# Second MLP products of a fp32 encoder: one of four weight sums and part of the common additions moved from VectorE to accumulating DMAs, and the third sum's split placed a pass earlier

## The chip, the cores and the metric

The kernel runs on one core of a Trainium2 chip. The metric is the device time of one execution in microseconds. Engines are named as in the profile: PE (TensorE matmul), PEld (its weight loads), DVE (VectorE), ACT (ScalarE), POOL (GpSimd) and SP (SyncE, which here only issues DMAs). DMAs are also issued from POOL's queue; those that accumulate into their destination are all issued there.

## The reference, cut to what matters

```python
D_MODEL = 1024; SEQ = 512; DEPTH = 2; D_FF = 4 * D_MODEL     # two sequences of 512 tokens

def sq_relu_mlp(h, w_up, w_down):
    a = jnp.maximum(h @ w_up, 0)
    return (a * a) @ w_down

def trunk(x, ...):
    for i in range(DEPTH):
        j = i // N_MIXERS
        if i % N_MIXERS == 0:
            x = x + fourier_mix(rms_norm(x, fourier_norm[j]), fourier_w_out[j])
        else:
            x = x + gqa_attention(rms_norm(x, attn_norm[j]), attn_w_qkv[j], attn_q_norm[j],
                                  attn_k_norm[j], attn_w_o[j])
        x = x + sq_relu_mlp(rms_norm(x, mlp_norm[i]), mlp_w_up[i], mlp_w_down[i])
    return rms_norm(x, final_norm)
```

All is float32. The change touches `(a * a) @ w_down`, the second product of the MLP, in both layers.

## The kernel before

**How a product is made.** A float32 matmul is done as three matmuls of float32r operands: each operand is split into an upper part (a cast, on ACT, line L82) and a lower part (value minus upper part, on DVE, line L83). `split`, `halves`, `load_w` and `load_raw` (whose DMA is issued on SP, line L91) do this for weights. `product` (matmuls at line L812) multiplies a 128x512 weight tile, as four k-blocks, with four 128x512 blocks of activations: 4 k-blocks times 3 matmuls, 12 matmuls of 512 columns.

**Seven products for eight.** The two sequences and the two halves of the 1024 outputs make a 2x2 block product, which is computed with seven block multiplications in the manner of Winograd. In `second_product(l, blocks, rows, late, ready)` two of the seven belong to class `Row` (first: weights a11, second: a12) and five to class `Sums`. The five `Sums` products of an output tile m (0 to 3) and a group g of k-blocks are s1·t1, s3·t3, s2·t2, s4·b22 and a22·t4, with weight sums s1 = a21 + a22, s2 = s1 - a11, s3 = a11 - a21, s4 = a12 - s2. The t and b are activation sums that the first product left in DRAM. `Sums.load` loads four weight blocks as two 512 KB transfers (x = a12, a21 and y = a11, a22, each block 128x512). `sum_123` makes s1, s2 and s3 by three DVE operations, L1126 to L1128, s1 and s2 in a buffer s of its own; `split_12`, `sum_4` (L1134), `split_4` and `split_3` follow (`split_3` splits s3 and a22, which stand side by side in y).

**The loop.** Each layer has 16 `items`: a `Sums` and the `Row`s due before it. One turn of the loop, a pass, runs the row's first product if there is one, then s1·t1, s3·t3, the row's second product, s2·t2, s4·b22 and a22·t4. A pass with a row has 84 matmuls, a pass without has 60; in layer 0 the last two passes have no row. After each product DVE adds the PSUM bank to an accumulator (L1059), which frees the bank. Meanwhile the next item is loaded (after s1·t1) and its sums and splits are made (after s2·t2 and s4·b22); only the third sum's split, `split_3`, stands at the start of the item's own pass. In layer 1 the sums of the first group are half as wide.

**What sets the order.** Within the loop only PE's order is the order of the code (`tc.manual_schedule(engines={PE})`); DVE, ACT, POOL and SP are ordered by a scheduler from the order of emission and readiness, and each then runs its own instructions strictly in that order. Raw weights live in 5 buffers of 128x1024 (`rawp`), taken round-robin: a load waits until the buffer's former content has been split or summed. Split weights have 4 buffers (`wp`), activations 38, short-lived tiles 8, PSUM 8 banks.

**The end of an output tile.** `e[m]` is a common part that goes to three of the four output blocks. When the last `Row` or `Sums` of m is through, `finish(m)` adds it: L1223 into the upper half of `xs[0, m]`, L1224 into both halves of `xs[1, m]`. Then `ready(m)` is called. In layer 0 it prepares the attention layer for the two sequences and two halves: `make_h` multiplies by a gain and splits (ACT L86, DVE L87), `square` squares (ACT L157) and adds (POOL L159), `put_away` stores `xs` to DRAM on SP (L186). `late()`, called in each of the last two passes of layer 0, loads and splits pieces of the attention's `w_qkv`. In layer 1 `ready` does nothing. In layer 0 the attention's projections (matmul lines L77 to L79) come after the last pass.

Of the kernel before, what the change touches and what calls it, by code (L numbers as in the profile page):

```python
# [11 lines left out]
F32 = mybir.dt.float32  # L12
# [3 lines left out]
ALU = mybir.AluOpType  # L16
AX = mybir.AxisListType

P = 128
# [21 lines left out]
def trunk_kernel(ctx, tc, x_in, xt_in, y_out, dcos, dsin, feat, rope, gfour, gcol, grow, gfin,  # L41
                 w_four, w_nyq, w_qkv, w_o, w_up, w_row2, w_row4, w_sum2, w_sum4, w_down):
    nc = tc.nc
# [3 lines left out]
    rawp = ctx.enter_context(tc.tile_pool(name="rawp", bufs=5))  # L47
# [9 lines left out]
    def nm(s):  # L57
        n_[0] += 1
        return f"{s}_{n_[0]}"

    def slot(shape, dt):
        return act.tile(shape, dt, tag="u4", name=nm("u"))

    def tm(shape=(P, 512), dt=F32):
        return tmp.tile(list(shape), dt, tag="t2", name=nm("t"))

    def small(n=4):
        return sm.tile([P, n], F32, tag="s", name=nm("s"), padded_shape=[P, 8])
# [20 lines left out]
    def load_raw(src, shape=(P, 1024)):  # L89
        raw = rawp.tile(list(shape), F32, tag="raw", name=nm("raw"))  # L90
        nc.sync.dma_start(raw, src)  # L91
        return raw
# [49 lines left out]
    xs, acc = {}, {}  # L142
# [9 lines left out]
    def square(q, fo, n=512):  # L152

        if fo == 0:
            acc[q] = tm()
        s = tm() if fo else acc[q]
        nc.scalar.activation(s[:, :n], xt(q, fo)[:, :n], AF.Square)  # L157
        if fo:
            nc.gpsimd.tensor_add(acc[q][:, :n], acc[q][:, :n], s[:, :n])  # L159
# [17 lines left out]
    def make_h(q, fo, g0):  # L177

        h = slot([P, 2, 512], F32R)
        split_scaled(h[:, 0], h[:, 1], xt(q, fo), gc[:, g0 + fo : g0 + fo + 1])  # L180
        return h
# [3 lines left out]
    def put_away(q, i):  # L185
        nc.sync.dma_start(park[q, i], xs[q, i])  # L186
# [390 lines left out]
    def even_outs(q, fos):  # L577
        return outs(q, fos, we, 0, 258, (wn.w, un[q]))
# [31 lines left out]
    with tc.manual_schedule(engines={ET.PE, ET.Activation, ET.DVE, ET.Pool, ET.SP}):  # L610
# [138 lines left out]
        for fo in range(KC):  # L749
            e, = even_outs(1, [fo])  # L750
# [289 lines left out]
    def second_product(l, blocks, rows, late=lambda: None, ready=lambda m: None):  # L1040
        e, new = [], [True] * 4
# [11 lines left out]
        def put(op, h):  # L1053
            for hi, lo in h:
                split(hi, lo, f32(lo))
            b[op] = b.get(op, []) + [(hi[:, i], lo[:, i]) for hi, lo in h for i in range(2)]
# [11 lines left out]
        def residual(q, m):  # L1068
            if (q, m) not in there:
                xs[q, m] = slot([P, 2, 512], F32)  # L1070
                nc.sync.dma_start(xs[q, m], park[q, m])
                there.add((q, m))
            return xs[q, m]
# [8 lines left out]
        def sums_raw(m, g, n):  # L1082
            if (1, m, g) in early:
                return early[1, m, g]
            w = w_sum4[3 * l + g, m] if n == 4 else w_sum2[m]
            return [load_raw(w[:, i : i + 2], (P, 2, n * P)) for i in (0, 2)]

        class Row:


            def __init__(self, m, g, n):
                self.m, self.g, self.n = m, g, n

            def load(self):
                residual(0, self.m)
                self.raw = None if self.m in rows_early else row_raw(self.m, self.g, self.n)
# [15 lines left out]
        class Sums:  # L1112


            def __init__(self, m, g, n):
                self.m, self.g, self.n, self.o = m, g, n, {}

            def load(self):
                for q in range(NSEQ):
                    residual(q, self.m)  # L1120
                self.x, self.y = sums_raw(self.m, self.g, self.n)

            def sum_123(self):
                a21, a11, a22 = self.x[:, 1], self.y[:, 0], self.y[:, 1]
                s = self.s = rawp.tile([P, 2, self.n * P], F32, tag="raw", name=nm("raw"))
                nc.vector.tensor_add(s[:, 1], a21, a22)  # L1126
                nc.vector.tensor_sub(s[:, 0], s[:, 1], a11)
                nc.vector.tensor_sub(a11, a11, a21)  # L1128

            def split_12(self):  # L1130
                self.s2, self.s1 = halves(self.s, self.n * P, (own, narrow)[self.n == 2])
# [31 lines left out]
        b, left = {}, [len(steps) // 4] * 4  # L1163
# [55 lines left out]

        def finish(m):  # L1220
            left[m] -= 1
            if left[m] == 0:
                nc.vector.tensor_add(xs[0, m][:, 1], xs[0, m][:, 1], e[m])  # L1223
                nc.vector.tensor_add(xs[1, m], xs[1, m], e[m].unsqueeze(1).broadcast_to([P, 2, 512]))  # L1224
                ready(m)

        first_product(l, blocks, rows, ahead)
        e += [tm() for _ in range(4)]
        items, waiting = [], []
        for _, i, m, g, n in sorted(steps):  # L1230
            if i:
                items.append((waiting, Sums(m, g, n)))
                waiting = []
# [5 lines left out]
        def change(op, i, g):  # L1239

            if g + 1 < len((ROW_GROUPS, SUM_GROUPS)[i][l]):
                later.append([0, op, g + 1, fetch(op, g + 1, (ROW_GROUPS, SUM_GROUPS)[i][l][g + 1][1])])

        if there_later:
            rows, sums = items[0]
            items[0] = [], sums
            with tc.manual_schedule(engines={ET.PE, ET.Activation, ET.DVE}):
                for r in rows:
                    r.load()
                    r.split()  # L1250
                sums.load()
                rows[0].first()
                rows[1].first()
                put(*there_later[0])
                sums.sum_123()
                sums.sum_4()
                rows[2].first()
                rows[3].first()
                for r, step in zip(rows, (sums.split_12, sums.split_4, sums.split_3, lambda: None)):
                    r.second()  # L1260
                    step()
                for r in rows:
                    finish(r.m)
        else:
            rows, sums = items[0]
            for r in rows:
                r.load()
                r.split()
            sums.load()
            sums.sum_123()  # L1270
            sums.split_12()
            sums.sum_4()
            sums.split_4()
            sums.split_3()
        def hook():
            for x in later:
                x[0] += 1
            if later and later[0][0] > 2:
                _, op, g, h = later.pop(0)
                b.pop(op, None)  # L1280
                put(op, h)
                held[op] = g

        for k, (rows, sums) in enumerate(items):
            nrows, nsums = items[k + 1] if k + 1 < len(items) else ([], None)
            if sums.g == len(SUM_GROUPS[l]) - 1 and sums.m > 1:
                late()
            with tc.manual_schedule(engines={ET.PE}):
                for r in rows:
                    r.first()  # L1290
                    if r.m == 3:
                        change("b11", 0, r.g)
                for r in nrows:
                    r.load()
                if k:
                    sums.split_3()
                hook()
                for i, op in enumerate(("t1", "t3", "t2", "b22", "t4")):
                    sums.go(i)
                    if sums.m == 3:  # L1300
                        change(op, 1, sums.g)
                    if i == 0 and nsums:
                        nsums.load()
                    if i == 1:
                        for r in rows:
                            r.second()
                            if r.m == 3:
                                change("b21", 0, r.g)
                        hook()
                        for r in nrows:  # L1310
                            r.split()
                    hook()
                    if there_later and k == 0 and i in (2, 4):
                        change(ROW[i // 4], 0, 0)
                    if i == 2 and nsums:
                        nsums.sum_123()
                        nsums.split_12()
                    if i == 3 and nsums:
                        nsums.sum_4()
                        nsums.split_4()  # L1320
            for r in rows:
                finish(r.m)
            finish(sums.m)


    hT, rs, wkv = [[], []], [], []
# [7 lines left out]
    def late():  # L1334
        for _ in range(2):
            wkv.append(load_w(w_qkv[2, len(wkv)], home=lent))

    def ready(m):
        for q in range(NSEQ):
            for fo in range(2 * m, 2 * m + 2):  # L1340
                hT[q].append(make_h(q, fo, KC))
                square(q, fo)
            put_away(q, m)
# [119 lines left out]
    for cg in (2, 0, 1):  # L1463
        ws = wkv if cg == 2 else [load_w(w_qkv[cg, u], home=own if u < 2 else lent) for u in range(4)]
        for q in range(NSEQ):
# [6 lines left out]
            for t in range(NT if (cg, q) != (1, 1) else 2):  # L1472
# [11 lines left out]
                if cg == 2:  # L1484
                    raw = tm((P, 256))
# [3 lines left out]
                else:  # L1489
                    raw = tm()  # L1490
# [7 lines left out]
    raw, ss = slot([P, 1024], F32), small(8)  # L1498
# [55 lines left out]
    for f in range(NF - 2 * NPS[1]):  # L1554
        raw = load_raw(plain[1][f], (P, 2, 512))
# [263 lines left out]
```

## Time and profile before

| what | value |
|---|---|
| median of 3 runs | 1739.89 us (1738.68 to 1741.07) |
| the profiled execution, its own time | 1740.44 us |
| its span | 1738.6 us |
| its mean granted TensorE clock | 0.992 |
| second product of layer 0 in the span | about 430 to 742 us |
| second product of layer 1 in the span | about 1420 to 1680 us |

Rows of the profile are read so. In the page's part on busy times, an engine's busy microseconds, share of the span and number of instructions. In a timeline, start and length in microseconds, engine, line, operation, destination and sources by name, shape, count of instructions that follow each other without a gap, and in brackets the idle time before them with what ended it. In the groups by line, after the bar: busy microseconds, mean nanoseconds of one, and the idle time before them. In the windows: for each stretch the busy time of each engine, the TensorE clock that was granted, the share of time in which the DMA engines were busy, and GB/s. In the DMA issues: count, size of one in KB, and microseconds from issue to landing.

### The profile page before, as it was taken

Reading aid. Unit: us, or ns where it says so; the run is one execution under the profiler, and the core shown is the slowest. Engines: PE = TensorE matmul, PEld = TensorE weight load, DVE = VectorE, ACT = ScalarE, POOL = GpSimd, SP = SyncE. Lnnn points to the kernel's source line nnn. Section 1 sums busy time; section 2 is a strip of 40 time slices with the busy share of each in tenths; the row PEclk is TensorE's granted clock in tenths of the full one; section 3 lists DMA queues with packets and bytes.
Section 4 is the critical chain, followed back from the end, with each engine's and each line's share of the span. In section 5 each row is a group of like instructions: output and inputs, shape, how many; then the busy total and the mean of one; then the engine's idle time right before and its main releaser. Section 6 shows DMA issues by size and latency. Waiting matters only on the chain. (4 is left out here: it accounts for less than half of the span.)

```text
span 1738.6 us, 21980 instructions
## 1 busy us (share of the span) xinstructions
PE 1685.3 (97%) x7870; PEld 1396.4 (80%) x7870; DVE 1250.9 (72%) x1855; ACT 871.2 (50%) x1530; POOL 349.8 (20%) x308
## 2 busy tenths in 40 slices
PE   4999999999999999999999999999999999999997
PEld 4887788888788888788877888787788878888886
DVE  8768776555878879975578843697745479787865
ACT  6666444545433434546687724554544554344334
POOL 3330444222000000412234302104332200000004
PEclk9999999999999999999999999999999999999999
DMA  9823455448754545420100213225544487455322
GB/s 281 234 93 121 159 195 192 152 182 286 277 180 159 194 144 195 156 106 25 49 25 1 97 49 120 90 101 188 199 157 151 172 313 265 147 207 186 127 74 97
DMA packets 103893, 267.11 MB, mean 154 GB/s; under 512 B 10200, under 2 KB 10200, under 8 KB 103784
## 3 DMA queue, kind: packets, MB, share of 16 engines
q1 hardware_dynamic: 87624, 233.73, 37.5%
q10 hardware_dynamic: 14112, 25.70, 3.9%
q0 software_dynamic: 2048, 6.29, 1.9%
q8 instruction: 61, 1.00, 0.2%
q14 instruction: 48, 0.39, 0.1%
HBM read 190.70 MB, written 73.92 MB: 152 GB/s over the span
## 5 line engine op out<-in xcount | busy, mean ns | idle before, releaser
L812 PE MATMUL ps<-u,w 128*128 128x512 f32 x4704 | 1083.9, 391 | 9.5 <-DVE w L83 5.0
L812 PEld LDWEIGHTS ps<-u,w 128*128 128x128 f32 x4704 | 882.5, 188 | 202.7 <-DVE t L889 7.8
L82 ACT CAST w<-raw 128x1024 fp32r<-128x1024 f32 (+1 forms) x226 | 219.6, 982 | 428.2 <-PE ps L812 268.4
L83 DVE TENSOR_TENSOR w<-raw,w 128x1024 fp32r<-128x1024 f32 (+1 forms) x226 | 260.1, 1153 | 54.7 <-ACT w L82 54.3
L159 POOL TENSOR_TENSOR t<-t,t 128x512 f32<-128x512 f32 (+1 forms) x56 | 80.2, 1436 | 734.1 <-ACT t L157 678.5
L83 DVE TENSOR_TENSOR u<-u,u 128x1024 fp32r<-128x1024 f32 x133 | 163.0, 1254 | 23.9 <-ACT u L82 23.9
L82 ACT CAST u<-u 128x1024 fp32r<-128x1024 f32 x133 | 133.3, 1043 | 72.7 <-PE ps L812 47.5
L77 PE MATMUL ps<-u,u 128*128 128x512 f32 (+2 forms) x424 | 162.6, 385 | 1.7 <-DVE u L604 0.9
L78 PE MATMUL ps<-u,u 128*128 128x512 f32 (+2 forms) x424 | 157.6, 372 | 5.7 <-DVE u L83 5.6
L79 PE MATMUL ps<-u,u 128*128 128x512 f32 (+2 forms) x424 | 157.9, 372 | 2.0 <-POOL u L83 1.5
L1059 DVE TENSOR_TENSOR u<-ps,u 128x512 f32<-128x512 f32 x160 | 109.8, 689 | 57.1 <-PE ps L812 56.1
L812 PE MATMUL ps<-u,u 128*128 128x512 f32 x528 | 126.9, 390 | 2.6 <-DVE t L900 1.8
L922 POOL TENSOR_TENSOR u<-u 128x512 f32<-128x512 f32 x28 | 36.1, 1289 | 414.9 <-ACT u L828 414.9
L812 PEld LDWEIGHTS ps<-u,u 128*128 128x128 f32 x528 | 98.6, 188 | 25.5 <-issue 2.9
L78 PEld LDWEIGHTS ps<-u,u 128*128 128x128 f32 x424 | 82.9, 195 | 18.0 <-DVE u L83 7.8
L79 PEld LDWEIGHTS ps<-u,u 128*128 128x128 f32 x424 | 82.5, 195 | 15.9 <-POOL u L83 2.1
L77 PEld LDWEIGHTS ps<-u,u 128*128 128x128 f32 x424 | 83.0, 196 | 13.8 <-ACT u L82 1.8
L83 DVE TENSOR_TENSOR u<-ps,u 128x512 fp32r<-128x512 f32 (+4 forms) x126 | 76.5, 627 | 17.8 <-ACT u L82 16.5
L885 DVE TENSOR_TENSOR t<-ps,u 128x512 f32<-128x512 f32 x30 | 20.8, 692 | 91.4 <-PE ps L812 89.9
L82 ACT CAST u<-ps 128x512 fp32r<-128x512 f32 (+4 forms) x126 | 66.5, 542 | 24.9 <-PE ps L79 14.2
L795 DVE TENSOR_TENSOR u<-ps,u 128x512 f32<-128x512 f32 (+1 forms) x48 | 30.9, 645 | 64.7 <-PE ps L79 64.7
L827 ACT ACTIVATE t<-t 128x512 f32<-128x512 f32 x60 | 37.8, 631 | 56.1 <-DVE t L900 45.4
(225 smaller groups left out, 2007.8 us busy)
## 6 DMA issues: line engine op xcount, KB each, us to landing
raw<-w_up SPq DMA_DIRECT2D x82, 512.0 KB, 3.9
u<-spill_t SPq DMA_DIRECT2D x60, 512.0 KB, 6.0
raw<-w_sum SPq DMA_DIRECT2D x56, 512.0 KB, 3.7
u<-spill_b SPq DMA_DIRECT2D x45, 512.0 KB, 5.6
spill_t<-u SPq DMA_DIRECT2D x87, 256.0 KB, 2.0
spill_b<-t ACTq DMA_DIRECT2D x60, 256.0 KB, 2.0
raw<-w_row SPq DMA_DIRECT2D x28, 512.0 KB, 3.5
park<-u SPq DMA_DIRECT2D x24, 512.0 KB, 3.2
```

Of the source, the lines that this page charges most:

```text
L77: nc.tensor.matmul(out, lh, rh, start=first, stop=False)
L78: nc.tensor.matmul(out, lh, rl, start=False, stop=False)
L79: nc.tensor.matmul(out, ll, rh, start=False, stop=last)
L82: nc.scalar.copy(dst_hi, src)
L83: eng.tensor_sub(dst_lo, src, f32(dst_hi))
L159: nc.gpsimd.tensor_add(acc[q][:, :n], acc[q][:, :n], s[:, :n])
L795: nc.vector.tensor_add(x[:, :n], o[:, :n], x[:, :n])
L812: nc.tensor.matmul(o, w[x][:, sl], h[k][y], start=first and k + i == 0, stop=k == n - 1 and i == 2, skip_group_check=not first)
L827: nc.scalar.activation(t, src, AF.Relu)
L885: nc.vector.tensor_add(u2, ob, t[:, 0])
L922: eng.tensor_sub(t[:, 0], b12, b11)
L1059: nc.vector.tensor_add(x, o, x)
```

## The change

Three things are changed in `second_product`.

1. `sums_raw` takes a third buffer, s, already when the weights are loaded. SP loads a21 into its half s[:, 1] (256 KB, half of that in the narrow group of layer 1), and POOL's queue issues an accumulating DMA that adds a22 from DRAM to it. So s1 is there without DVE. a21 and a22 are read from DRAM a second time. `sum_123` becomes `sum_23`: s3 = a11 - a21 in place, then s2 = a22 - s3, which is the same sum.
2. In layer 0, for m below 3, `finish` issues two accumulating DMAs on POOL's queue (SBUF to SBUF, 256 KB and 512 KB) in place of the DVE additions L1223 and L1224. For m = 3 and in layer 1 the DVE additions stay. `ready(m)` is called one pass later for m below 3, by a list `done`.
3. `split_3` moves from the start of an item's own pass to the end of the pass before it (after a22·t4).

```diff
@@ sums_raw
-            return [load_raw(w[:, i : i + 2], (P, 2, n * P)) for i in (0, 2)]
+            s = rawp.tile([P, 2, n * P], F32, tag="raw", name=nm("raw"))
+            nc.sync.dma_start(s[:, 1], w[:, 1])
+            nc.gpsimd.dma_start(s[:, 1], w[:, 3], accum_op=ALU.add)
+            return [s] + [load_raw(w[:, i : i + 2], (P, 2, n * P)) for i in (0, 2)]
...
@@ Sums
-                self.x, self.y = sums_raw(self.m, self.g, self.n)
-
-            def sum_123(self):
+                self.s, self.x, self.y = sums_raw(self.m, self.g, self.n)
+
+            def sum_23(self):
                 a21, a11, a22 = self.x[:, 1], self.y[:, 0], self.y[:, 1]
-                s = self.s = rawp.tile([P, 2, self.n * P], F32, tag="raw", name=nm("raw"))
-                nc.vector.tensor_add(s[:, 1], a21, a22)
-                nc.vector.tensor_sub(s[:, 0], s[:, 1], a11)
                 nc.vector.tensor_sub(a11, a11, a21)
+                nc.vector.tensor_sub(self.s[:, 0], a22, a11)
...
@@ finish(m)
-            if left[m] == 0:
+            if left[m]:
+                return
+            both = e[m].unsqueeze(1).broadcast_to([P, 2, 512])
+            if m < 3 and l == 0:
+                nc.gpsimd.dma_start(xs[0, m][:, 1], e[m], accum_op=ALU.add)
+                nc.gpsimd.dma_start(xs[1, m], both, accum_op=ALU.add)
+            else:
                 nc.vector.tensor_add(xs[0, m][:, 1], xs[0, m][:, 1], e[m])
-                nc.vector.tensor_add(xs[1, m], xs[1, m], e[m].unsqueeze(1).broadcast_to([P, 2, 512]))
-                ready(m)
+                nc.vector.tensor_add(xs[1, m], xs[1, m], both)
+            done.append(m)
...
@@ the loop over items
                 for r in nrows:
                     r.load()
-                if k:
-                    sums.split_3()
                 hook()
...
+                    if i == 4 and nsums:
+                        nsums.split_3()
                     hook()
...
             finish(sums.m)
+            while done and (done[0] < sums.m or done[0] == 3):
+                ready(done.pop(0))
```

More of the change, by code (lines that the diff above doesn't have):

```diff
@@ L1221, in finish @@
             left[m] -= 1
-            if left[m] == 0:
+            if left[m]:
[5 more added lines that the diff above has]
+            else:
                 nc.vector.tensor_add(xs[0, m][:, 1], xs[0, m][:, 1], e[m])
-                nc.vector.tensor_add(xs[1, m], xs[1, m], e[m].unsqueeze(1).broadcast_to([P, 2, 512]))
-                ready(m)
+                nc.vector.tensor_add(xs[1, m], xs[1, m], both)
+            done.append(m)
         first_product(l, blocks, rows, ahead)
         e += [tm() for _ in range(4)]
-        items, waiting = [], []
+        items, waiting, done = [], [], []
         for _, i, m, g, n in sorted(steps):
@@ L1254, in second_product @@
                 put(*there_later[0])
-                sums.sum_123()
+                sums.sum_23()
                 sums.sum_4()
@@ L1269, in second_product @@
             sums.load()
-            sums.sum_123()
+            sums.sum_23()
             sums.split_12()
@@ L1315, in second_product @@
                     if i == 2 and nsums:
-                        nsums.sum_123()
+                        nsums.sum_23()
                         nsums.split_12()
```

## The prediction

> **What bounds the kernel now.** The page first: its head and the busy times.
> ```profile
> span 1738.6 us, 21980 instructions
> PE 1685.3 (97%) x7870; PEld 1396.4 (80%) x7870; DVE 1250.9 (72%) x1855; ACT 871.2 (50%) x1530; POOL 349.8 (20%) x308
> ```
> PE is busy in 97% of the span, so work taken off DVE is worth only what it takes out of PE's gaps. How many of those lie in the second products is read from the view of windows; its columns are stretch, length, busy time and count of PE, PEld, DVE, ACT, POOL, the granted clock, DMA share and GB/s.
> ```profile
> 450.00:500.00 50.00, 49.00 (x215) 39.83 (x214) 39.45 (x50) 14.74 (x16) 0.00 (x0) 1.00 0.45 167
> 550.00:600.00 50.00, 50.00 (x222) 41.43 (x221) 39.04 (x48) 20.41 (x22) 0.00 (x0) 1.00 0.57 201
> 700.00:750.00 50.00, 46.17 (x195) 37.38 (x195) 47.56 (x51) 25.65 (x36) 16.98 (x10) 0.97 0.51 185
> 1400.00:1450.00 50.00, 49.14 (x215) 39.71 (x214) 38.47 (x64) 22.79 (x35) 0.00 (x0) 1.00 0.82 292
> ```
> A full window holds 222 matmuls, that is 0.2267 us of PE for one. Between the ends of a second product PE is full; the shortfalls stand at three places: start of layer 0, end of layer 0 (clock 0.97, DVE 95% busy), start of layer 1. Next the timeline of PE there (start, length, line, count, idle before and its releaser):
> ```profile
> 430.27 39.03 PE L812 MATMUL ps<-u,w 128*128 128x512 f32 x170
> 470.30 13.90 PE L812 MATMUL ps<-u,w 128*128 128x512 f32 x60 [1.00 <-DVE w L83]
> ...
> 725.08 3.02 PE L812 MATMUL ps<-u,w 128*128 128x512 f32 x12 [1.52 <-DVE w L83]
> 730.41 12.36 PE L812 MATMUL ps<-u,w 128*128 128x512 f32 x46 [2.31 <-DVE w L83]
> 742.61 0.39 PE L77 MATMUL ps<-u,u 128*128 128x512 f32 x1
> ...
> 1429.60 3.06 PE L812 MATMUL ps<-u,u 128*128 128x512 f32 x12 [0.83 <-DVE u L1059]
> ```
> Layer 0's start: 170 x 0.2267 = 38.54 us after 430.27 is 468.81; the next group begins at 470.30, so 1.5 us are lost. Its end: the last pass has five products, 60 matmuls, 13.60 us. It could start at 725.08 - 1.52 = 723.56 and end at 737.16; the following stage begins at 742.61, so 5.45 us are lost. Two stalls make 3.83 of it. Most of the rest is the clock, by two-microsecond windows:
> ```profile
> 732.00:734.00 2.00, 2.00 (x6) 1.55 (x5) 2.00 (x2) 2.00 (x4) 1.92 (x3) 0.50 0.94 324
> ```
> Half clock for 2 us costs 1.0 us. Layer 1's start loses 0.83. The change can win at most 1.5 + 5.45 + 0.83 = 7.8 us.
>
> What holds s1 and s3 of the last pass is on the timelines of DVE, ACT and POOL:
> ```profile
> 719.85 1.21 DVE L83 TENSOR_TENSOR u<-raw,u 128x1024 fp32r<-128x1024 f32 x1
> 722.72 2.30 DVE L83 TENSOR_TENSOR w<-raw,w 128x1024 fp32r<-128x1024 f32 x1
> 726.14 1.21 DVE L1224 TENSOR_TENSOR u<-u,t 128x1024 f32<-128x1024 f32 x1
> 727.88 0.74 DVE L87 SCALAR_TENSOR_TENSOR u<-u,gc,u 128x512 fp32r<-128x512 f32 x1
> 728.54 0.68 DVE L1223 TENSOR_TENSOR u<-u,t 128x512 f32<-128x512 f32 x1
> 729.14 1.22 DVE L83 TENSOR_TENSOR w<-raw,w 128x1024 fp32r<-128x1024 f32 x1
> ...
> 716.10 1.05 ACT L82 CAST w<-raw 128x1024 fp32r<-128x1024 f32 x1
> 721.77 1.04 ACT L82 CAST w<-raw 128x1024 fp32r<-128x1024 f32 x1
> ...
> 721.94 2.00 POOL L159 TENSOR_TENSOR t<-t,t 128x512 f32<-128x512 f32 x1 [3.76 <-ACT t L157]
> ```
> ACT had the upper half for s1 at 717.15; DVE came to the lower half at 722.72 and took 2.30 us beside POOL's addition, where the same shape takes 1.22 alone. For s3 ACT was done at 722.81, and DVE began at 729.14, behind L1224, L87 and L1223. So it is DVE's queue.
>
> **The change part by part.** *Removed from DVE:*
> ```profile
> L1126 DVE TENSOR_TENSOR raw<-raw,raw 128x512 f32<-128x512 f32 (+1 forms) x32 | 21.0, 656 | 7.9 <-DMA raw<-w_sum 7.6
> ```
> All 32 additions of L1126 (21.0 us) and, in layer 0 for three of four m, three of L1223 and three of L1224 (0.68 and 1.21 in the rows above, 3 x 1.89 = 5.7 us) go: 26.7 us of DVE. In full windows DVE has 22% idle, so there this is worth nothing.
>
> *Added:* 32 loads of half the size on SP, and 38 accumulating DMAs issued by POOL. The view of DMA issues (KB each, median us to landing) and that of one line bound them:
> ```profile
> raw<-w_sum SPq DMA_DIRECT2D x8, 256.0 KB, 5.2
> u<-u POOLq DMA_DIRECT2D x4, 256.0 KB, 4.3
> raw<-w_four POOLq DMA_DIRECT2D x3, 512.0 KB, 5.7
> u<-xt POOLq DMA_DIRECT2D x4, 512.0 KB, 7.8
> L387 POOL DMA_DIRECT2D u<-u x4: 855/865/888, 51.9 to 66.3; - x4
> ```
> All three POOL rows are accumulating DMAs: 256 KB from SBUF to SBUF (L387) 4.3 us, 512 KB from DRAM 5.7 and 7.8. So an accumulate lies between 4.3 and 7.8. I take 4.3 for 256 KB and 5.7 for 512 KB, because the sizes are the same and the 7.8 stood in the crowded first stage. The instruction holds POOL 0.87 us.
>
> The Trainium skill, "DMA: Bandwidth & Descriptors", section "Anatomy of one DMA — SWDGE (gpsimd) path", fits a POOL-issued DMA at 2.0 us plus its bytes over 436 GB/s; an estimate by it is 2.6 us for 256 KB. The 4.3 measured is longer, and the sum goes by that.
>
> *Steady state, layers 0 and 1.* Timelines of DVE and ACT:
> ```profile
> 558.08 0.69 DVE L1126 TENSOR_TENSOR raw<-raw,raw 128x512 f32<-128x512 f32 x1 [0.17 <-DMA raw<-w_sum]
> 561.63 0.69 DVE L1134 TENSOR_TENSOR raw<-raw,raw 128x512 f32<-128x512 f32 x1
> ...
> 568.10 1.05 ACT L82 CAST w<-raw 128x1024 fp32r<-128x1024 f32 x1 [9.78 <-PE ps L812]
> ...
> raw<-w_sum SPq DMA_DIRECT2D x56, 512.0 KB, 3.7
> ```
> The sums are done at 562.3, their first split starts at 568.10: 5.8 us of cover. The last load landed at 558.1, so it was issued near 554.4. The new half-load takes the buffer that the row before it gave up, and stands ahead of the other two on SP, so it goes out no later: load 5.2, POOL 0.9, accumulate 4.3 put it at 564.8; with 7.8 at 568.3. Cover 3.3 us, or 0.2 short. Only the split needs that half. The third load, whose buffer now comes free at the previous fourth sum's split rather than before, lands some 1.4 us later (estimate: one 128x1024 split and its neighbour), inside the 5.8. Bounds 0 to 0.2 x some 24 passes = +5; I take **0**. In the 550 window DMA share is 0.57, and a pass's extra 512 KB of packets fit.
>
> *Start of layer 0.* Around the stall at 470.30 DVE did:
> ```profile
> 461.35 0.69 DVE L1126 TENSOR_TENSOR raw<-raw,raw 128x512 f32<-128x512 f32 x1
> 467.29 1.22 DVE L83 TENSOR_TENSOR u<-u,u 128x1024 fp32r<-128x1024 f32 x1
> 468.42 1.82 DVE L83 TENSOR_TENSOR w<-raw,w 128x512 fp32r<-128x512 f32 x2
> ```
> The split that PE awaited ended at 470.24. In the changed build L1126 is gone from that chain (0.60 us of pitch) and the split of 467.29 (1.13 of pitch) stands behind the third sum's split: 1.73 us against a stall of 1.5. Bounds 0 (a half-load that lands late gives it back) to -1.5; I take **-1.4**.
>
> *End of layer 0.* Unstalled, the last pass wants s1 at 723.6, s3 at 726.3, s2 at 729.0, s4 at 731.7, a22 at 734.5. I walked the changed build's queues with the durations above and these, of DVE and ACT:
> ```profile
> 704.80 0.69 DVE L83 TENSOR_TENSOR w<-raw,w 128x512 fp32r<-128x512 f32 x1
> ...
> 711.74 0.73 ACT L86 ACTIVATE u<-u,gc 128x512 fp32r<-128x512 f32 x1 [3.83 <-DVE u L1223]
> 712.90 0.71 ACT L86 ACTIVATE u<-u,gc 128x512 fp32r<-128x512 f32 x1
> ```
> The last sums' third load goes out when the fourth sum's split before it is done (705.5 here, and 1.2 later for the third sum's split now ahead of it) and lands 3.7 us after, at 710.4. A difference (0.6), the third split of m = 2's pass (1.2), a difference and m = 1's last addition follow: 713.4. POOL issues both accumulates then, the 512 KB first: it lands at 719.2 (5.7), the 256 KB one, which ACT needs first, at 713.5 + 0.87 + 4.3 = 718.7. ACT's gain and square pairs (1.16 apart) stand behind that landing, and behind them, in ACT's order, its part of s4 and s3 of the last pass; three pairs and four copies (3.5 + 3.7) give 725.9. DVE's s3 split, once 729.14, now follows at 726.3 and, with POOL's squares beside it (2.30), ends by 728.6: 2.3 late instead of 4.1. s1 is in time: nothing of m = 2 stands ahead of its split, so its 1.5 goes. What is late next: a split of w_qkv stands ahead of the addition that frees s4's bank (0.4), and the gain multiplications of m = 2, waiting for the second pair of accumulates, stand ahead of the one that frees a22's (0.5). With one stall of that size instead of two I count no half clock. Left 2.3 + 0.4 + 0.5 = 3.2 of 5.45: **-2.2**. Bounds: -5.45 if each accumulate lands in time, and +7 at 7.8 us (under the third rival).
>
> A rule of the Trainium skill bears on the 2.30 us row: "SBUF — State Buffer", section "Who interferes with whom", says that a DVE operation with two SBUF inputs and a GpSimd operation that reads SBUF lock each other out for the whole instruction. The row, 2.30 beside POOL's addition against 1.22 alone, agrees; as the squares on POOL stay, the rule leaves this cost where it is.
>
> *Start of layer 1.*
> ```profile
> 1425.59 0.42 DVE L1126 TENSOR_TENSOR raw<-raw,raw 128x256 f32<-128x256 f32 x1 [2.72 <-DMA raw<-w_sum]
> 1428.86 0.69 DVE L1059 TENSOR_TENSOR u<-ps,u 128x512 f32<-128x512 f32 x1
> ```
> The addition at 1428.86 freed the bank of the stall; one operation of 0.42 ahead of it goes. But that chain begins with a load that was 2.72 us late, with DMA at 0.82, and the new order waits for one load more and a buffer that the first split frees. Bounds -0.8 to +3; I take **-0.3**, nearest to the removed row.
>
> *Moving the third sum's split* to the end of the previous pass removes no instruction; PE's order is unchanged, and it is what puts that split ahead of m's finishing work, counted above. Sum: -1.4 - 2.2 - 0.3 = **-3.9**. The profiled execution has 1740.44 us (span 1738.6), so 1736.5; the median of the runs is 0.55 below that execution, so **1736.0**.
>
> **The rivals.**
> 1. *All three stalls go*: -7.8, about 1732.1. For it: no stall had another releaser than DVE. Against it: new waits on landings stand in ACT's and DVE's queues. By the fit of the Trainium skill, "DMA: Bandwidth & Descriptors", named above, landings of 2.6 us would come 1.7 earlier.
> 2. *It moves and nothing comes of it*: the half-load and accumulate at the two starts land as late as the additions were, and the end keeps a stall of the same size in another place, or the work was hidden and the stall belonged to POOL's squares (2.30 row). Without the gain at the end it is -1.7, 1738.2; between 1737 and 1741.
> 3. *The accumulates land late, slower*: ACT takes its work in order, so a landing one microsecond later makes s3's split one later, delays m = 2's last addition and through it the second pair, and so s4 and a22 too: some 2.7 us per us (estimate: s3, a22, and 0.7 for the clock, which fell to 0.50 after the two stalls here). From 4.3 + 2.2 / 2.7 = 5.1 us for the 256 KB one on, the end of layer 0 loses; at 7.8 it is 3.5 x 2.7 - 2.2 = +7.2. With -1.4 and -0.3 that is +5.5, near 1745.4. For it: the 7.8 of one row, and that each pair shares a queue and 768 KB. In the steady state the same landing adds up to +5. Against it: two of the three rows are at 4.3 and 5.7, and the DMA share of the 700 window is 0.51.
>
> **How the numbers follow.** Forecast 0.38, with its own range 1733.5 to 1738.5; first rival 0.18, second 0.18, third 0.26. A measurement of this kernel can tell 0.2%, 3.5 us, from no change, so faster means below 1736.4 and slower above 1743.4. The forecast stands close to the first bound. Faster: 0.22 of the forecast, 0.18, 0.02 of the second = 0.42. Same: 0.16, 0.14 and 0.05 = 0.35. Slower: 0.02 of the second and 0.21 of the third = 0.23. The range goes from just under the first rival to just over the third's price: 1731 to 1746; what lies outside is a third rival with the steady state's loss.
>
> **What would show it.** After: PE's gap near 470 gone; in the last pass of layer 0 a gap at s3 of about 2.3 and none at s1; the granted clock there at 1.00; accumulates landing at 4.3 (256 KB) and 5.7 (512 KB); full windows still at 222 matmuls; DVE 26 to 27 us less busy. Wrong would be: gaps in the middle windows, released by a DMA or an ACT split (a late half-load); 256 KB landings above 5.1 us; a longer idle at the start of layer 1; or ACT waiting for the accumulates while PE waits for s1.

## The result and the profile after

The changed kernel took 1753.02 us (median of 4 runs, 1752.02 to 1754.24) against 1740.48 us for the kernel before in the same runs: ratio 1.0075, 95% interval 1.0063 to 1.0087. It is slower by 12.5 us, where 1736.0 was forecast. The third rival gave 1745.4, and the measured time lies beyond it and beyond the range.

The page's head and busy times of the changed kernel, its queues (packets, MB, share of 16 engines), and its windows, in the columns used above:
```profile
span 1750.6 us, 22155 instructions
PE 1689.6 (97%) x7870; PEld 1398.1 (80%) x7870; DVE 1225.3 (70%) x1817; ACT 869.5 (50%) x1530; POOL 381.5 (22%) x346
...
q1 hardware_dynamic: 92232, 241.59, 40.0%
q0 software_dynamic: 7904, 16.52, 5.3%
```
```profile
450.00:500.00 50.00, 50.00 (x222) 41.40 (x221) 38.60 (x48) 16.82 (x18) 3.46 (x4) 1.00 0.67 216
550.00:600.00 50.00, 50.00 (x222) 41.39 (x221) 37.64 (x46) 19.89 (x21) 2.61 (x3) 1.00 0.69 217
700.00:750.00 50.00, 38.40 (x150) 29.28 (x149) 35.52 (x38) 22.55 (x33) 18.96 (x16) 0.93 0.70 205
1400.00:1450.00 50.00, 48.91 (x213) 39.31 (x212) 35.26 (x54) 24.81 (x39) 3.48 (x4) 1.00 0.95 315
```
DVE is 25.6 us less busy, and that bought nothing: the window at 700 did 150 matmuls where it had done 195. Its 45 missing matmuls are 10.2 us. The window at 450 is full now (222 for 215), the one at 550 stayed full, the one at 1400 has two fewer. So nearly the whole loss stands at the end of layer 0. The timeline of PE there:
```profile
427.62 2.97 PE L812 MATMUL ps<-u,u 128*128 128x512 f32 x12 [0.53 <-DVE t L900]
...
705.94 6.58 PE L812 MATMUL ps<-u,w 128*128 128x512 f32 x26 [0.61 <-DVE u L1059]
716.23 15.87 PE L812 MATMUL ps<-u,w 128*128 128x512 f32 x60 [3.70 <-DVE w L83]
734.55 8.29 PE L812 MATMUL ps<-u,w 128*128 128x512 f32 x34 [2.45 <-DVE w L83]
747.50 5.49 PE L812 MATMUL ps<-u,w 128*128 128x512 f32 x12 [4.66 <-DVE u L1059]
752.79 0.63 PE L77 MATMUL ps<-u,u 128*128 128x512 f32 x1
```
Gaps of 0.61 + 3.70 + 2.45 + 4.66 = 11.4 us stand where the kernel before had 1.52 + 2.31. The first and the last row give a measure that leaves out what varies elsewhere between executions, and all runs below are read by it: the time from the 12 matmuls released by L900, at the beginning of layer 0's second product, to the first projection. Here it is 752.79 - 427.62 = 325.17 us. In the kernel before it was 742.61 less the start of this row, 315.15 us:
```profile
427.46 2.97 PE L812 MATMUL ps<-u,u 128*128 128x512 f32 x12 [0.54 <-DVE t L900]
```
This **stage time** grew by 10.0 us; the rest, from the first projection to the end of the span, grew from 995.99 to 997.81, which lies within what it varies by between the runs below (995.3 to 998.4 in all but one).

What stands behind the gaps is in ACT's line of the view of waits over 690 to 755 us, and in the DMA issues of the changed kernel (KB each, median us to landing):
```profile
ACT u L86 <- DMA u<-t: 18.6, 3, 7.5
```
```profile
raw<-w_sum POOLq DMA_DIRECT2D x28, 256.0 KB, 6.3
u<-t POOLq DMA_DIRECT2D x3, 512.0 KB, 8.5
u<-u POOLq DMA_DIRECT2D x4, 256.0 KB, 3.9
u<-t POOLq DMA_DIRECT2D x3, 256.0 KB, 7.4
```
ACT waited 18.6 us in three waits for the accumulates of `finish` (u<-t). They landed after 7.4 and 8.5 us (medians; 5.9 to 8.1 and 7.0 to 8.9), not 4.3 and 5.7. The older accumulate, u<-u at the kernel's beginning, still landed in 3.9.

The first of the three waits makes the gap of 3.70, two short passes later. Rows of POOL, ACT, DVE and SP of the changed kernel, in order of time:
```profile
690.15 0.92 POOL L1228 DMA_DIRECT2D u<-t  x1 [1.45 <-DVE u L1059]
697.62 0.72 ACT L86 ACTIVATE u<-u,gc 128x512 fp32r<-128x512 f32 x1 [7.46 <-DMA u<-t]
704.71 2.51 ACT L82 CAST w<-raw 128x1024 fp32r<-128x1024 f32 x3
707.05 2.73 SPq L91 DMA_DIRECT2D raw<-w_sum  x2
709.94 0.68 DVE L83 TENSOR_TENSOR w<-raw,w 128x512 fp32r<-128x512 f32 x1
714.35 0.69 DVE L1129 TENSOR_TENSOR raw<-raw,raw 128x512 f32<-128x512 f32 x1 [3.13 <-DMA raw<-w_sum]
714.96 1.22 DVE L83 TENSOR_TENSOR w<-raw,w 128x1024 fp32r<-128x1024 f32 x1
```
The second accumulate of m = 0 (L1228, 256 KB) was issued at 690.15 and had landed by 697.6; ACT stood still for 7.46 us with the gain of m = 0 at the head of its queue. Behind that work stood two `w_qkv` splits and the three splits of the last but one pass, which ACT reached only at 704.71. The last sums' loads need buffers that those splits free; the second went out at about 709.4 and DVE's first difference (L1129) waited for it until 714.35. Behind that difference, in DVE's order, stood the third split of the last but one pass, which ended at 716.18; PE went on at 716.23. The run e3 below, which has no accumulates in `finish` and is otherwise the changed kernel, shows the same instructions without ACT's wait:
```profile
699.34 2.72 SPq L91 DMA_DIRECT2D raw<-w_sum  x2
706.26 0.69 DVE L1129 TENSOR_TENSOR raw<-raw,raw 128x512 f32<-128x512 f32 x1 [2.75 <-DMA raw<-w_sum]
```
There the second of the two loads went out near 701.7, 277.0 us after the beginning of the stage (424.74 in e3); in the changed kernel it is 281.8 us after it, 4.8 us later.

The waits of m = 1 (5.83 us, until 723.73) and m = 2 (5.30 us, until 743.65) lead in the same way to the gaps of 2.45 and 4.66, the last of them straight: the gain multiplications on DVE stood ahead of the addition that frees a bank.

### The profile page after: what moved, and what is told of

Same layout as the page of the kernel before. It is cut to its first block, busy times and chain, and to the rows that moved or that the text cites. A ratio compares the mean times of both kernels' runs of the same rounds, so it can differ in the third digit from the quotient of the medians.

```text
span 1750.6 us, 22155 instructions
## 1 busy us (share of the span) xinstructions
PE 1689.6 (97%) x7870; PEld 1398.1 (80%) x7870; DVE 1225.3 (70%) x1817; ACT 869.5 (50%) x1530; POOL 381.5 (22%) x346
## 3 DMA queue, kind: packets, MB, share of 16 engines
q1 hardware_dynamic: 92232, 241.59, 40.0%
q0 software_dynamic: 7904, 16.52, 5.3%
## 5 line engine op out<-in xcount | busy, mean ns | idle before, releaser
L1088 POOL DMA_DIRECT2D raw<-w_sum x32 | 27.7, 867 | 491.8 <-DVE w L83 248.1
L82 ACT CAST u<-ps 128x512 fp32r<-128x512 f32 (+4 forms) x126 | 66.5, 543 | 24.3 <-PE ps L79 14.1
```

The costliest lines, as they stand in the source:

```text
L82: nc.scalar.copy(dst_hi, src)
L1088: nc.gpsimd.dma_start(s[:, 1], w[:, 3], accum_op=ALU.add)
```

## The experiments

All medians below stand beside runs of the kernel before on the same chip, and the ratios are to those.

| run | what it has | stage time, us | first projection to end, us | ratio to before, 95% interval |
|---|---|---|---|---|
| before | | 315.15 | 995.99 | 1 |
| after | all of the change | 325.17 | 997.81 | 1.0075 (1.0063 to 1.0087) |
| e1 | sums by DMA, early split | 309.87 | 996.96 | 0.9992 (0.9982 to 1.0002) |
| e2 | finish alone | 322.79 | 995.67 | 1.0049 (1.0033 to 1.0066) |
| e3 | all, but DVE adds in finish | 311.04 | 996.72 | 0.9998 (0.9983 to 1.0012) |
| e4 | early split alone | 310.92 | 996.16 | 0.9988 (0.9978 to 0.9997) |
| e5 | finish, early split | 322.73 | 995.34 | 1.0066 (1.0050 to 1.0083) |
| e6 | finish, sums by DMA | 325.23 | 998.42 | 1.0080 (1.0058 to 1.0101) |
| e7 | all, but POOL adds in finish | 311.88 | 998.37 | 1.0006 (0.9995 to 1.0016) |
| e8 | all, accumulates for m = 0 alone | 315.27 | 996.11 | 1.0019 (1.0007 to 1.0032) |
| e9 | all, the 256 KB accumulates alone | 316.73 | 996.47 | 1.0029 (1.0017 to 1.0040) |
| e10 | sums by DMA in layer 0, early split | 309.88 | 997.30 | 0.9981 (0.9973 to 0.9990) |
| e11 | all, ready later still | 312.37 | 1003.85 | 1.0009 (0.9998 to 1.0021) |

The stage times are single profiled executions, and those of e3 and e9 were the fastest of their runs, that of e11 the slowest. For the large steps the medians, each less its kernel before, say the same: the change lies 13.1 us above e3, 13.1 above e7 and 14.9 above e1, e8 lies 4.1 above e3, and e9 5.8. For the small ones they don't: e3 has 4.1 us less than before in the stage and 0.5 less in the median, e4 4.2 and 2.5. So steps of one or two us in the stage time are an indication only.

**Which part: e1 to e4.** e1 undoes only `finish`:
```diff
-            if m < 3 and l == 0:
-                nc.gpsimd.dma_start(xs[0, m][:, 1], e[m], accum_op=ALU.add)
-                nc.gpsimd.dma_start(xs[1, m], both, accum_op=ALU.add)
-            else:
+            if left[m] == 0:
                 nc.vector.tensor_add(xs[0, m][:, 1], xs[0, m][:, 1], e[m])
                 nc.vector.tensor_add(xs[1, m], xs[1, m], both)
-            done.append(m)
+                ready(m)
```


> The changed kernel with finish as before (DVE additions, ready at once); the weight sum by DMA and the early third split stay. Theory 1 (the accumulates of finish land late and ACT and DVE stand behind them): the loss of 12.5 us goes, the start of layer 0 keeps its 1.5 us, so 1735 to 1740 us, and no gap over 2 us in the last three passes of layer 0 but those of before. Theory 2 (the new half-load of the sums shifts the buffers round so that the last sums wait for the w_qkv splits): most of the loss stays, 1748 us or more, with DVE's difference of the last sums waiting for a load.

It took 1737.07 us, as expected by theory 1, and the loss is gone. e2 is the opposite, the kernel before with that part of the diff alone.

> The kernel before with only finish changed (accumulating DMAs for m below 3 in layer 0, ready one pass later). Theory 1: 1749 to 1755 us, ACT waiting 15 to 20 us for u<-t accumulates. Theory 2: 1738 to 1743 us.

It took 1747.92 us: slower, by less than expected, with ACT waiting 20.5 us. Two thirds of the loss (8.5 of 12.5 us) come with this part by itself. e3 tells the landing from the lateness of `ready`:
```diff
-            if m < 3 and l == 0:
-                nc.gpsimd.dma_start(xs[0, m][:, 1], e[m], accum_op=ALU.add)
-                nc.gpsimd.dma_start(xs[1, m], both, accum_op=ALU.add)
-            else:
-                nc.vector.tensor_add(xs[0, m][:, 1], xs[0, m][:, 1], e[m])
-                nc.vector.tensor_add(xs[1, m], xs[1, m], both)
+            nc.vector.tensor_add(xs[0, m][:, 1], xs[0, m][:, 1], e[m])
+            nc.vector.tensor_add(xs[1, m], xs[1, m], both)
             done.append(m)
```


> The changed kernel with DVE additions in place of the accumulates of finish, but ready still called one pass later. If it is the landing (theory 1): 1734 to 1740 us. If it is the lateness of ready, whose work then falls into the last two short passes: 1746 us or more. Theory 2: 1748 us or more.

1738.90 us and a stage of 311.04: calling `ready` a pass later costs little (1.2 us of stage against e1, where it is called at once); the accumulates cost the rest. e4 moves only the split in the kernel before:
```diff
-                if k:
-                    sums.split_3()
...
+                    if i == 4 and nsums:
+                        nsums.split_3()
```


> The kernel before with only the third split moved to the end of the pass before. Theories 1 and 2: 1735 to 1741 us, the stall at s3 of the last pass of layer 0 (2.3 us) gone or under 1 us. If the moved split itself did the harm (ahead of the additions that free banks): 1744 us or more.

1736.94 us, and its timeline of PE has one gap left in the last pass:
```profile
470.68 253.26 PE L812 MATMUL ps<-u,w 128*128 128x512 f32 x1116 [1.01 <-DVE w L83]
725.46 13.44 PE L812 MATMUL ps<-u,w 128*128 128x512 f32 x58 [1.52 <-DVE w L83]
738.74 0.39 PE L77 MATMUL ps<-u,u 128*128 128x512 f32 x1
```
The gap of 2.31 at s3 is gone, with all of DVE's additions still in place, and s1's 1.52 is untouched. So s3 was late because its split stood behind the finishing work in DVE's order, not because DVE had those additions to do. The stage is 4.2 us shorter: 2.31 for the gap and most of the rest for the clock, which held 1.00 (last section). The run as a whole is 2.5 us faster than before, 0.12%.

**What the sums by DMA have to do with it: e5 and e6.** Finish alone adds 7.6 us to the stage, the whole change 10.0, though its other parts alone save 5.3. e5 adds the early split to e2 (e2 and e4's diffs together); e6 is the changed kernel with the split back in its place.

> The kernel before with the accumulates of finish (ready one pass later) and the early third split, the weight sums on DVE. Read by the stage from the 12 matmuls released by L900 to the first projection matmul: before 315.15 us, changed kernel 325.17, accumulates of finish alone 322.79, early split alone 310.92. Theory 1a (what the changed kernel loses beyond finish alone comes from the sums' DMAs: their buffer is one that a w_qkv piece holds, whose split stands on ACT behind the wait for the accumulates): 317 to 320 us, that is finish alone less what the early split wins. Rival 1b (it comes from the early split): 324 us or more.

> The changed kernel with the third split back at the start of the pass. Theory 1a: 324 to 329 us in that stage, with DVE waiting for a load of the last sums for over 2 us and ACT for u<-t accumulates for 16 to 20. Rival 1b: 317 to 321 us.

e5 had 322.73 us, between the two expectations: the early split gains nothing once ACT stands before it, and does no harm. e6 had 325.23, and its first long gap is again near that of the changed kernel, 3.76 for 3.70, where e5 has 0.83:
```profile
714.60 8.00 PE L812 MATMUL ps<-u,w 128*128 128x512 f32 x34 [0.83 <-DVE w L83]
```
```profile
713.78 16.80 PE L812 MATMUL ps<-u,w 128*128 128x512 f32 x60 [3.76 <-DVE w L83]
```
So in the stage time the added 2.4 us come with the sums' DMAs and not with the split: the two runs with both stand at 325.2, the two with the accumulates alone at 322.8. The medians can't tell these runs apart (e5 and e6 lie 11.2 and 12.6 us above before, with overlapping intervals). PE's gaps add up to 10.6 us in e5 and in e6 alike, since the sums' DMAs take away the 1.00 at the start of the stage; what is added is mostly the clock behind the gap of 3.76, which was 0.50, 0.50 and 0.51 in the windows from 714 to 720, 3.0 us. That the buffers of the last sums are the way to that gap is read from the chain above, and wasn't tried by itself. The DMA engines are another way, since the landings of u<-t (median, 256 and 512 KB) were 5.6 and 6.8 us without the sums' DMAs in e5 and 6.9 and 8.3 with them in e6.

**Landing, or leaving DVE: e7.**
```diff
-                nc.gpsimd.dma_start(xs[0, m][:, 1], e[m], accum_op=ALU.add)
-                nc.gpsimd.dma_start(xs[1, m], both, accum_op=ALU.add)
+                for x in (xs[0, m][:, 1], xs[1, m][:, 0], xs[1, m][:, 1]):
+                    nc.gpsimd.tensor_add(x, x, e[m])
```


> The changed kernel with three additions of 128x512 on POOL in place of the two accumulating DMAs. If the landing is what costs (256 KB in 7.4 us and 512 KB in 8.5 in the changed kernel, against some 4 to 5 us for three POOL additions): 312 to 319 us in that stage. If it costs that the work left DVE for any slower path: 322 us or more.

The same additions, off DVE, on the same queue, and the stage is 311.88 us. POOL takes 1.66 us for one (median; 1.28 to 2.29), some 5 us for the three, and it starts each when its operand is there:
```profile
683.72 1.28 POOL L1229 TENSOR_TENSOR u<-u,t 128x512 f32<-128x512 f32 x1 [4.76 <-DVE t L1059]
686.76 1.66 POOL L1229 TENSOR_TENSOR u<-u,t 128x512 f32<-128x512 f32 x1 [1.76 <-DVE u L1059]
689.04 1.30 POOL L1229 TENSOR_TENSOR u<-u,t 128x512 f32<-128x512 f32 x1 [0.62 <-DVE u L1059]
```
The last ends at 690.34, 1.3 us after its operand. The accumulate issued at 690.15 in the changed kernel landed 7.4 later. So the price is the landing, and not that the sum is computed off DVE.

**Which m: e8 and e9.** e8 keeps the accumulates for m = 0 (`if m == 0 and l == 0`), e9 only the smaller one of each m:
```diff
                 nc.gpsimd.dma_start(xs[0, m][:, 1], e[m], accum_op=ALU.add)
-                nc.gpsimd.dma_start(xs[1, m], both, accum_op=ALU.add)
+                nc.vector.tensor_add(xs[1, m], xs[1, m], both)
```


> The changed kernel with accumulates for m = 0 alone, DVE additions for m = 1 and 2 (ready one pass later for all three). Theory 1: every accumulate costs where ACT meets it; the waits of m = 1 and m = 2 go and with them the gaps of 2.45 and 4.66 us, m = 0's stays with the 3.70 one behind it: 313 to 318 us in that stage. If m = 0's is harmless, since it has a whole long pass to land in: 309 to 312 us.

```profile
714.75 15.23 PE L812 MATMUL ps<-u,w 128*128 128x512 f32 x60 [3.40 <-DVE w L83]
731.56 10.99 PE L812 MATMUL ps<-u,w 128*128 128x512 f32 x46 [1.58 <-DVE w L83]
```
e8's stage is 315.27 us, 4.2 above e3, which has none: m = 0 by itself brings the first gap, and m = 1 and 2 make the other 9.9 of the 14.1 by which the changed kernel lies above e3.

> The changed kernel with only the 256 KB accumulate of finish left on POOL's queue, the 512 KB one back as a DVE addition. Stage as before (changed kernel 325.17 us, before 315.15). If the landing of 7.4 us came from the pair (the 256 KB one issued behind 512 KB on the same queue): landing 3.9 to 4.5 us, as L387's, and 316 to 320 us. If it is the path at this place: landing 5.5 to 8 us, and 320 to 324 us.

The 256 KB accumulate without its neighbour landed in 3.8 to 6.2 us, median 5.9, so neither expectation holds whole: its landing is that of the second, its stage that of the first. The neighbour is worth some 1.5 of the 7.4. Why the 256 KB take 5.9 here and 4 at the kernel's beginning is open. The stage is 316.73 us, 5.7 above e3 for 256 KB in place of 768.

**Standing behind them, or their traffic: e11.**
```diff
-            while done and (done[0] < sums.m or done[0] == 3):
+            while done and (done[0] < sums.m - 1 or 3 in done):
```


> The changed kernel with ready called two passes later for m = 0 and after the last pass for m = 1 to 3. Theory 1 (the accumulates cost because ACT and DVE stand behind them in order, not because of their traffic): ACT waits for u<-t under 4 us in all, the gaps of 3.70 and 2.45 us in the last two passes go; the heaped work then delays the projections, so 312 to 320 us in the stage or up to 10 us more behind it. If the traffic on the DMA engines is what costs: 323 us or more in the stage with gaps in the last two passes still behind DVE's weight splits.

All accumulates are there, nothing waits for them until later, and the stage falls to 312.37 us with none of the gaps of 3.70, 2.45 and 4.66; one of 2.14 and one of 0.51 are left. ACT still waited 8.5 us for u<-t, more than expected: 3.09 for m = 0, 0.69 for m = 1, and 4.75 after its last weight split of the stage. Behind the stage this execution is 7.9 us longer than before. PE's waits until 1440 show 5.2 of it (10.6 us for 5.4); only 1.6 of that stands right behind the stage, before 800, so that the heap of finishing work makes all of it is not shown. The run as a whole, 1741.39 us, can't be told from before.

**The better version: e10.** e1 with sums by DMA only in layer 0 (layer 1 as before):
```diff
+            if l:
+                return [None] + [load_raw(w[:, i : i + 2], (P, 2, n * P)) for i in (0, 2)]
             s = rawp.tile([P, 2, n * P], F32, tag="raw", name=nm("raw"))
```


> Early third split, weight sums by DMA in layer 0 alone, finish as before. From the stage times so far: 309 to 311 us in the stage, 995.3 to 996.5 us from the first projection to the end (996.1 to 998.4 in the six runs with the sums by DMA in layer 1 too, 995.3 to 996.2 in the four without), so some 6 us less than the kernel before: 1733 to 1736 us. If layer 1's sums by DMA cost nothing: as the run with both layers, 1737 us.

1735.58 us, ratio 0.9981 (0.9973 to 0.9990): 3.6 us faster than before, and faster than the changed kernel. It can't be told from e4's one moved line (2.5 us) nor from e1 (2.4), whose intervals overlap with its own. The reason given for it doesn't hold: the rest after the first projection is 997.30, as with the sums by DMA in both layers, so no cost of layer 1's DMAs is shown. It has e1's stage, 309.88, with the first gap of layer 0 gone and two small ones at the end:
```profile
725.21 0.73 PE L812 MATMUL ps<-u,w 128*128 128x512 f32 x2 [0.29 <-ACT w L82]
727.03 10.73 PE L812 MATMUL ps<-u,w 128*128 128x512 f32 x46 [1.09 <-DVE w L83]
```

## Why the prediction was wrong, point by point

- **What bounds the kernel** was right: DVE's 25.6 us bought nothing in full windows, and only the three places could move. Its 0.2267 us for one matmul doesn't follow from the window (50 / 222 = 0.2252), but from long rows (253.26 / 1116 = 0.2269 in e4); no term hangs on the difference.
- **Steady state at 0** was right. The sums' accumulates landed in 6.3 us, not 4.3; the 2.0 us more fit in the 3.3 of cover that were worked out, and the middle windows kept 222 matmuls. The sums' plain loads of 512 KB took longer too, 5.5 us for 3.7, and the cover held that as well. So the loss beyond the range didn't come as the prediction put it, by "a third rival with the steady state's loss": the steady state lost nothing.
- **Start of layer 0, -1.4**, was right: in every run with the sums by DMA the gap near 470 is gone. Against e4, e1 has 1.05 us less in the stage, and the window at 450 holds 7 matmuls more, 1.6 us.
- **Start of layer 1, -0.3**: the idle went from 0.83 to 1.01 us. Over all runs PE's gaps from 1420 to 1470 us add up to between 0 and 1.56 us with layer 1's sums on DVE (five runs, mean 0.5) and to between 0 and 3.07 with them by DMA (eight runs, mean 1.2). So a gain there is not shown.
- **End of layer 0, -2.2**, is the step that failed, at +11 (16.5 us lost there for 5.45, worked out below), by two terms. First, the size of the landing: "I take 4.3 for 256 KB and 5.7 for 512 KB" took rows of the beginning of the kernel; they were 7.4 and 8.5, beyond the 5.1 from which the prediction itself let the end of layer 0 lose. The third rival had the mechanism: at 7.4 its estimate gives (7.4 - 4.3) x 2.7 - 2.2 = +6.2; no run varied the landing alone, so its slope is not shown. Second, a wait left out: the walk began with m = 1 and took the last sums' third load to go out at 705.5 + 1.2, from the timeline of before, and to land 3.7 later. The pair of m = 0 isn't in it, and so was costed at nothing without a reason; it held ACT for 7.46 us and put that load off to about 709.4, and the load took 4.9 us. By itself this pair costs 4.2 us (e8 against e3). The estimate and this wait make +10.4 of the 11.
- **"It is what puts that split ahead of m's finishing work, counted above"**: the gain at s3 was counted with the accumulates. e4 shows that the moved split wins it alone, with DVE's additions in place. The accumulates add nothing to it (e3, which has none of them, has 311.04).
- **"s1 is in time"** holds: in the last pass of the changed kernel no gap stands before s1, but the pass before it lost 3.70. "I count no half clock" was wrong: windows of the changed kernel from 746 to 754 have 0.71, 0.50, 0.50 and 0.58, 2 x (0.29 + 0.50 + 0.50 + 0.42) = 3.4 us, and the pair below 1.7:
```profile
716.00:718.00 2.00, 1.77 (x4) 1.48 (x5) 2.00 (x5) 1.05 (x1) 0.21 (x1) 0.53 0.98 203
718.00:720.00 2.00, 2.00 (x7) 1.53 (x7) 1.76 (x2) 0.00 (x0) 0.70 (x1) 0.61 0.85 253
...
748.00:750.00 2.00, 2.00 (x6) 1.52 (x6) 2.00 (x2) 1.28 (x3) 1.94 (x2) 0.50 0.59 242
750.00:752.00 2.00, 2.00 (x7) 1.52 (x6) 2.00 (x3) 0.99 (x1) 1.36 (x1) 0.50 0.00 0
```
  With 11.4 us of gaps these 5.1 make 16.5 us at the end of layer 0, where the kernel before lost 5.45.
- **Against the third rival** stood "two of the three rows are at 4.3 and 5.7". Those rows stood in another stage, and ACT had waited for one of them only once, 2.0 us (L528); nothing in them spoke for a landing at the end of layer 0. The DMA share of the 700 window rose from 0.51 to 0.70 with the change's own traffic. The fit of the Trainium skill, "DMA: Bandwidth & Descriptors", section "Anatomy of one DMA — SWDGE (gpsimd) path", gives 2.6 us for 256 KB; the 7.4 measured is nearly three times that.

## What to carry to other kernels

Moving an addition from a busy engine to a DMA traded about a microsecond of that engine for a landing of 6 to 9 us here, and the engine that consumed the result in order stood still for it, with all that was queued behind; so first look at what stands behind the consumer, for each place where it happens, the one with the most slack too. When an operand is late because its instruction stands in the wrong place of an engine's queue, move that instruction: one moved line here won as much of the stage as the removed work was to win. Try the parts of a change apart: of three, one won 4.2 us of stage time, one about 1, and one lost 7.6 by itself and 15.3 in company.

## What the runs showed of the hardware

The packets of POOL's queue used the DMA engines about twice as long per byte as those of SP's: in the changed kernel 5.3% for 16.52 MB, 0.32% per MB, against 40.0% for 241.59 MB, 0.17%. All but 1.05 MB of POOL's were accumulating. Whether the accumulating costs this or the queue, no run here tells.

The clock falls behind a gap of PE, but these runs show no one length from which it does. In the last passes of layer 0, all eight gaps from 3.23 to 5.12 us were followed by two-microsecond windows down to 0.50 to 0.55 (3.23 in e9, 3.40 in e8, 3.70 and 4.66 in the changed kernel, 3.76 and 5.12 in e6, 3.98 in e2, 5.04 in e5). Single gaps of 1.52 (e4), 1.58 (e8) and 1.85 us (e7) were followed by 1.00. In between it went both ways: 1.00 behind 2.31 (e9), 2.45 (the changed kernel), 2.46 (e5) and 2.92 us (e3), but 0.50 behind 2.14 (e11) and 2.42 us (e2), as behind the pair of 1.52 and 2.31 in the kernel before. e2 and e5 have the same pattern, a gap of 1.3 us, 6.2 us of matmuls and a gap of 2.42 or 2.46, and only e2's clock fell. Here are e3 and e11, each with its gap and a window behind it:
```profile
724.95 10.99 PE L812 MATMUL ps<-u,w 128*128 128x512 f32 x46 [2.92 <-DVE w L83]
726.00:728.00 2.00, 2.00 (x10) 1.66 (x9) 2.00 (x3) 1.43 (x4) 0.00 (x0) 1.00 0.80 287
```
```profile
713.96 25.95 PE L812 MATMUL ps<-u,w 128*128 128x512 f32 x106 [2.14 <-DVE w L83]
716.00:718.00 2.00, 2.00 (x6) 1.52 (x6) 2.00 (x3) 0.46 (x1) 0.43 (x1) 0.50 1.03 297
```
Between 121 and 126 us of the span each run has a gap of 1.5 us, and within 4 us behind it the clock was at 0.50 to 0.59 in all but e3. So the length of the last gap alone doesn't decide it, and what else does is open. The Trainium skill, "TensorE: Matmul & The Clock Gate", section "What's actually happening", names an idle window of about 3.4 us for the fall. The gaps of 3.23 us and more agree with it within a few tenths; the falls behind 2.14 and 2.42 us do not.
